# Where the matmul operands lie in SBUF, modulo 256 bytes: level with the weights, or 64 bytes behind them

## The chip, the cores and the metric

The kernel runs on one core of a Trainium2 chip. A core has a matrix engine (TensorE, in the profile PE for the matmuls and PEld for the loads of their stationary operands), VectorE (DVE), ScalarE (ACT), GpSimd (POOL) and DMA queues, here those of SyncE (SP), which bring the weights from device memory into SBUF, the on-chip memory of 128 partitions. An address in this text is a byte offset within each partition. The metric is the device time of one execution in microseconds (us), the median over runs.

## The reference, cut to what matters

The reference is a decoder trunk of two layers on 256 positions of width 2048, in float32. Each layer has a mixer and a dense feed-forward with hidden width 8192, each wrapped in norms and a residual:

```
for layer in range(2):
    y = rmsnorm(h, norm_w[layer, 0])
    y = linear_attention_mixer(y, ...) if layer == 0 else spatial_gating_mixer(y, ...)
    h = h + rmsnorm(y, norm_w[layer, 1])
    y = square(relu(rmsnorm(h, norm_w[layer, 2]) @ w_up)) @ w_down
    h = h + rmsnorm(y, norm_w[layer, 3])
```

The mixer of layer 0 projects 2048 to 8208 columns, runs a gated delta rule and a retention on 8 heads each, and projects back. The mixer of layer 1 projects 2048 to 8192 columns, gates the halves against each other over blocks of 128 positions (a LayerNorm and eight 128x128 matrices) and projects 4096 back to 2048. Nearly all the arithmetic is in the products with the large weights.

## The kernel before, in words

**Products of float32 in three matmuls.** Every float32 operand of a large product is split in two: `hi`, rounded to the engine's reduced float32 form (float32r), and `lo`, the rest. A product is hi·hi + lo·hi + hi·lo, three matmuls that add into one PSUM bank (lines 138 to 140, 324 to 326 and 368 to 370). For each matmul the engine first loads a 128x128 stationary operand (its first argument, PEld in the profile), then streams the moving operand (its second argument) of 256 or 512 columns through the array. Each matmul of these lines has a load of its own, and the load for the next matmul runs while the present one streams.

**Weights.** `weights` (line 121) brings a unit of 128x2048 numbers, 1 MB, by one DMA into a tile `raw`, ScalarE copies it rounded into `whi` (line 131), and VectorE writes the rest to `wlo` (line 132). There are 3 buffers of `raw` and 4 each of `whi` and `wlo`, 8192 bytes in a partition each.

**Three kinds of large product.**

- `chunk_tok` (line 161): activations stationary, 128 positions at a time, and 512 columns of weights moving (`prod_tok`, lines 138 to 140). All projections of the mixers, part of the down projection of the feed-forwards and the first chunk of each up projection go this way. In layer 0 a few products have 400, 384 or 256 columns. With 400 columns (line 500, `spans0`) a unit holds four blocks of 1600 bytes, and block j of the moving weights begins 64·j bytes (modulo 256) behind the first.
- `up_pass` (line 313): weights stationary, and all 256 positions of the normed activations `xh`, `xl` moving (lines 324 to 326). Fifteen of the sixteen chunks of each up projection go this way.
- `chunk7` (line 355): 512x512 blocks of the down projection by seven half-size products in place of eight (sums of operand blocks are formed on VectorE), with the hidden activations `e0`, `e1` or their sums `f0`, `f1` stationary and 256 columns of weights or weight sums moving (lines 368 to 370). One `chunk7` has 7·2·3 = 42 matmuls, and 37 of them run in each feed-forward.

**Between the stages.** `down_last` (line 256) finishes a sub-layer: it adds the last products, norms, adds to the residual `h`, and writes the input of the next sub-layer, transposed and split, into eight tiles `xh0` to `xh3`, `xl0` to `xl3` of pool `xp`. `new_x` (line 207) takes these tiles; each has 4 k-tiles of 256 positions, 4096 bytes.

**Where tiles lie.** Pools are laid one behind the other: `gap` (one tile of `PAD0` bytes, only there to move what follows), `wp` (weights), `cp` (small constants, beginning with a second tile of `PAD1` bytes), `xp` (normed activations), `hp` (residual and accumulators), and then the pool of the running stage: `l0`, `ffn1`, `sg`, `ffn3`. In the program as built, modulo 256 bytes: `raw`, `whi` and `wlo` begin at 0; all `xh`, `xl` at 0; the feed-forward's `e0`, `e1`, `f0`, `f1`, `qsum`, `rl`, `tr` at 0; in layer 1's mixer `v0` to `v7` at 128 and `e0` to `e3` at 0; in layer 0's mixer `kq`, `Bn`, `PT` at 0 and `Um0`, `Um1` at 224. Slices that the matmuls take out of these tiles begin at multiples of 512 bytes in them, except in the products of 400 columns. In layer 1's mixer the tiles `v0` to `v7` hold the value half first and are then used again, beside `e0` to `e3`, for the gated activations that are the stationary operands of the output projection.

**Order.** The order within each engine comes from the code above and the tile framework's scheduler; tensors wait for each other by semaphores.

Of the kernel before, what the change touches and what calls it, by code (L numbers as in the profile page):

```python
# [10 lines left out]
F32 = mybir.dt.float32  # L11
F32R = mybir.dt.float32r
# [5 lines left out]
P = 128  # L18
D = 2048
SEQ = 256  # L20
# [9 lines left out]
PARTS = [4, 2, 1, 1]  # L30
WAIT = [26, 30]
AHEAD = 200
PAD0, PAD1 = 896, 544
WARM = 10
SEVEN, KEPT = (0, 1, 2), 1
ORDER = (None, 0, None, 1, None, 2, None, 3)
# [59 lines left out]
def program(tc, nc, A, S):  # L96
# [3 lines left out]
    xp = tc.alloc_tile_pool(name="xp", bufs=1)  # L100
# [5 lines left out]
    V, G, ACT, PE, DMA = nc.vector, nc.gpsimd, nc.scalar, nc.tensor, nc.sync  # L106
    uid = [0]
    ahead = [0]

    V.memset(gap.tile([P, PAD0 // 4], F32, tag="gap0", name="gap0"), 0.0)  # L110
    V.memset(cp.tile([P, PAD1 // 4], F32, tag="gap1", name="gap1"), 0.0)

    def T(pool, shape, tag, dt=F32, bufs=None):
        uid[0] += 1
        kw = {} if bufs is None else {"bufs": bufs}
        return pool.tile(shape, dt, tag=tag, name=f"{tag}_{uid[0]}", **kw)
# [81 lines left out]
            ACT.activation(hi, src, AF.Copy, scale=col)  # L198
            V.scalar_tensor_tensor(lo, src, col, hi.bitcast(F32), ALU.mult, ALU.subtract)

    def group(pool, th, tl, bufs=None):
        return T(pool, [P, 4, SEQ], th, F32R, bufs), T(pool, [P, 4, SEQ], tl, F32R, bufs)

    def kts(groups):
        return [(e[0][:, j, :], e[1][:, j, :]) for e in groups for j in range(4)]

    def new_x(n=4):
        return [group(xp, f"xh{g}", f"xl{g}") for g in range(n)]

    def to_channels(src, dst, b, col=None):  # L210
        tp = bank(tpp, 512, "tp")
# [28 lines left out]
    h = [[None] * 4 for _ in range(2)]  # L240
# [14 lines left out]

    def down_last(s, X, rows, w1, w0, yw, rpend):
        units = [weights(s, [(r, [(c * 512, 512)]) for r in rows]) for c in range(4)]
        newx = None if w0 is None else new_x()
        rh = [None, None]
        rv = [None, None]  # L260
        for b in range(2):
            ssy = small(4, "ssy")
            yb = yw(b)
            for c in range(4):
                ps = bank(acc, 512, "acc")
                for j in range(4):
                    prod_tok(ps, X[j], b, units[c], j, 512, j == 0, j == 3)
                yt = y[b][c]
                V.tensor_tensor(yt, ps, yt, ALU.add)  # L269
                square_sum(ssy[:, c : c + 1], yt)  # L270
                (V if c == 3 else G).tensor_tensor(yb[c], yt, w1[c], ALU.mult)  # L271
                if c == 2:
                    base = small(1, "base")
                    V.tensor_reduce(base, ssy[:, 0:3], AX.X, ALU.add)
                    V.tensor_scalar(base, base, 1.0 / D, EPS if rpend is None else rpend[b], ALU.mult, ALU.add)
            rs = small(1, "rs")
            V.tensor_scalar(rs, ssy[:, 3:4], 1.0 / D, base, ALU.mult, ALU.add)
            rsqrt(rs, rs)
            for c in range(4):
                ht = h[b][c]  # L280
                V.scalar_tensor_tensor(ht, yb[c], rs, ht, ALU.mult, ALU.add)  # L281
                if w0 is None:
                    DMA.dma_start(A["out"][b * P : (b + 1) * P, c * 512 : (c + 1) * 512], ht)
                else:
                    (V if c == 0 else G).tensor_tensor(yb[c], ht, w0[c], ALU.mult)
                    to_channels(yb[c], newx[c], b)
        if w0 is not None:
            for b in range(2):
                ssh = small(4, "ssh")
                for c in range(4):  # L290
                    square_sum(ssh[:, c : c + 1], h[b][c])
                rh[b] = T(cp, [P, 1], f"rh{b}", bufs=2)
                tot = small(1, "tot")
                V.tensor_reduce(tot, ssh, AX.X, ALU.add)
                var = small(1, "var")
                V.tensor_scalar(var, tot, 1.0 / D, EPS, ALU.mult, ALU.add)
                rsqrt(rh[b], var)
                rv[b] = T(cp, [P, 1], f"rv{b}", bufs=2)
                V.tensor_scalar(rv[b], var, var, EPS, ALU.mult, ALU.mult)
            newx = kts(newx)  # L300
        return newx, rh, rv
# [81 lines left out]
    def ffn(up, dn, X, rh, w1i, w0i):  # L383
        last = HID // 512 - 1
        with tc.tile_pool(name=f"ffn{w1i}", bufs=1, reuse_waits="tile") as fp:

            def pair(name):
                return T(fp, [P, 4, SEQ], f"{name}h", F32R), T(fp, [P, 4, SEQ], f"{name}l", F32R)

            def relu2(ps):  # L390
                r = T(fp, [P, 512], "rl", bufs=3)
# [65 lines left out]
            t = []  # L457
# [36 lines left out]
    def layer0_mixer():  # L494
        rstd = [T(cp, [P, 1], f"rh{b}", bufs=2) for b in range(2)]
        s = S["la_in"]
        with tc.tile_pool(name="l0", bufs=1, reuse_waits="tile") as lp:
            xg = new_x()
            X = kts(xg)
            spans0 = [(4096, 16), (3072, 384)]  # L500
            ps = [bank(acc, 400, "acc") for _ in range(2)]
# [512 lines left out]
    def layer1_mixer(X, rh):  # L1014
        si, so = S["sg_in"], S["sg_out"]
        with tc.tile_pool(name="sg", bufs=1, reuse_waits="tile") as gp:
            ws = T(gp, [P, 8, P], "ws")
            DMA.dma_start(ws, A["ws"].rearrange("p (g t) -> p g t", t=P))
            G.affine_select(ws, ws, pattern=[[0, 8], [1, P]], compare_op=ALU.is_ge, fill=0.0, base=0,
                            channel_multiplier=-1)  # L1020
            v = [None] * 8
            st = [T(gp, [P, 8, 6], f"st{b}") for b in range(2)]

            def v_evac(c, b, ps):
                if v[c] is None:
                    v[c] = T(gp, [P, 2, 512], f"v{c}")
                ACT.activation(v[c][:, b, :], ps, AF.Gelu_apprx_tanh, scale=rh[b])
                V.bn_stats(st[b][:, c, :], v[c][:, b, :])

            for b, ps in first_chunk(si, X, [(SGW, 512)]):  # L1030
                v_evac(0, b, ps)
            for c in range(1, 8):
                ps = chunk_tok(si, X, ALLK, [(SGW + c * 512, 512)], 512)
                for b in range(2):
                    v_evac(c, b, ps[b])
            rs, mu = [], []
            for b in range(2):
                mv = T(gp, [P, 2], f"mv{b}")
                V.bn_aggr(mv, st[b])
                var = small(1, "var")  # L1040
                V.tensor_scalar(var, mv[:, 1:2], EPS, None, ALU.add)
                r = T(gp, [P, 1], f"lr{b}")
                rsqrt(r, var)
                rs.append(r)
                mu.append(mv[:, 0:1])

            tags = ["e0", "e1", "e2", "e3", "v0", "v1", "v2", "v3", "e0", "e1", "e2", "e3", "v4", "v5", "v6", "v7"]
            gts = [None] * 8

            def gate(g):  # L1050
                wb = T(hp, [P, 512], "bc", bufs=4)
                DMA.dma_start(wb, A["lnw"][:, g * 512 : (g + 1) * 512].partition_broadcast(P))
                bb = T(hp, [P, 512], "bc", bufs=4)
                DMA.dma_start(bb, A["lnb"][:, g * 512 : (g + 1) * 512].partition_broadcast(P))
                pss = []
                for b in range(2):
                    t = v[g][:, b, :]
                    V.tensor_scalar(t, t, mu[b], rs[b], ALU.subtract, ALU.mult)
                    G.tensor_tensor(t, t, wb, ALU.mult)
                    G.tensor_tensor(t, t, bb, ALU.add)  # L1060
                ps = chunk_tok(si, X, ALLK, [(g * 512, 512)], 512)
                us = []
                for b in range(2):
                    pm = bank(mxp, 512, "mx")
                    PE.matmul(pm, ws[:, g, :], v[g][:, b, :], start=True, stop=True)  # L1065
                    u = T(gp, [P, 512], "u", bufs=2)
                    ACT.activation(u, ps[b], AF.Gelu_apprx_tanh, scale=rh[b])
                    V.scalar_tensor_tensor(u, pm, bsc[:, g : g + 1], u, ALU.add, ALU.mult)
                    us.append(u)
                dst = (T(gp, [P, 4, SEQ], tags[2 * g], F32R), T(gp, [P, 4, SEQ], tags[2 * g + 1], F32R))  # L1070
                for b in range(2):
                    blocks_split(T(hp, [P, 512], "bc", bufs=4), us[b], dst, b)
                gts[g] = kts([dst])

            def rows(g):
                return [g * 512 + j * P for j in range(4)]

            gate(0)
            for a in (0, 2, 4):
                gate(a + 1)  # L1080
                gate(a + 2)
                down(so, gts[a] + gts[a + 1], rows(a) + rows(a + 1), a == 0)
            gate(7)
            down(so, gts[6], rows(6), False)

            def rows_in(tags):
                t = [T(gp, [P, 2, 512], g) for g in tags]
                return [t[0][:, 0], t[0][:, 1], t[1][:, 0], t[1][:, 1]]

            w1 = row_load(rows_in(["v0", "v1"]), "nrow", 2)  # L1090
            w0 = row_load(rows_in(["v2", "v3"]), "nrow", 6)
            return down_last(so, gts[7], rows(7), w1, w0, lambda b: rows_in(["e0", "e1"]), None)
# [62 lines left out]
```

## Time and profile before

| | |
|---|---|
| median of 2 runs | 2518.86 us (2517.79 to 2519.94) |
| profiled execution | 2520.84 us, span 2519.1 us |
| granted TensorE clock, mean | 0.998 |
| PE busy | 2485.1 us, 99% of the span, 15418 matmuls |
| PEld busy | 2234.5 us, 89% |
| DVE / ACT / POOL busy | 1984.7 (79%) / 1260.5 (50%) / 183.2 us (7%) |
| DMA | 480.17 MB, mean 191 GB/s |

A busy share is the part of the span in which an engine worked. The end of a matmul in this profile is modelled, and a row's mean duration of a matmul is longer than the time from its start to the start of the next: matmuls overlap in the pipeline. What a stream of matmuls costs is read from the starts.

By time the program runs as follows: layer 0's mixer until about 565 us, its feed-forward until about 1250 us, layer 1's mixer until about 1815 us, its feed-forward until the end.

### The profile page before, as it was taken

The numbers are of one execution on the slowest core, as the hardware profiler recorded it, in microseconds if no ns is written. First come the engines' busy times: TensorE is split into PE (matmuls) and PEld (weight loads), VectorE is DVE, ScalarE is ACT, GpSimd is POOL, SyncE is SP. The second block draws the span as 40 slices with busy tenths as digits, with TensorE's granted clock in tenths as the row PEclk, the third lists the DMA queues.
The fourth block names the chain that finished last, engine by engine and source line by source line (L and its number), as shares of the span: only waits on it lengthen the run. The fifth ranks groups of instructions, "written<-read, shape, count | busy, mean of one in ns | idle before, by whom it ended". The sixth has DMA issues, their size and how long they took to land.

```text
span 2519.1 us, 37114 instructions
## 1 busy us (share of the span) xinstructions
PE 2485.1 (99%) x15418; PEld 2234.5 (89%) x15418; DVE 1984.7 (79%) x2322; ACT 1260.5 (50%) x1266; POOL 183.2 (7%) x144
## 2 busy tenths in 40 slices
PE   9999999999999999999999999999999999999998
PEld 8788888879999999999878878888799999999997
DVE  6586855578898889889864596876888988988897
ACT  6655444455455545455554434333555545555553
POOL 0001201130000000000210110110300000000001
PEclk9999999999999999999999999999999999999999
DMA  8444544644554555555455455555445555555553
GB/s 310 164 154 152 191 157 175 213 159 184 204 190 180 197 200 193 192 202 203 182 218 188 181 208 209 196 197 200 151 185 202 189 194 201 201 184 184 201 203 132
DMA packets 81832, 480.17 MB, mean 191 GB/s; under 512 B 13696, under 2 KB 15872, under 8 KB 27392
## 3 DMA queue, kind: packets, MB, share of 16 engines
q1 hardware_dynamic: 81664, 477.80, 52.5%
q8 instruction: 121, 1.98, 0.3%
q14 instruction: 47, 0.39, 0.0%
HBM read 475.14 MB, written 2.62 MB: 190 GB/s over the span
## 4 chain that ended last, share of the span: by engine, by line
PE 46%; DVE 3%; POOL 1%; issue 0%; ACT 0%; DVEq 0%; POOLq 0%; ACTq 0%
PE acc L138 8%; PE acc L140 8%; PE acc L139 8%; PE tp L326 5%; PE tp L325 5%; PE tp L324 5%; PE acc L368 1%; PE acc L370 1%; PE acc L369 1%; PE mx L370 1%; PE mx L369 1%; PE mx L368 1%; DVE h L281 1%; DVE wlo L132 1%; PE mx L1065 1%
## 5 line engine op out<-in xcount | busy, mean ns | idle before, releaser
L132 DVE TENSOR_TENSOR wlo<-raw,whi 128x2048 fp32r<-128x2048 f32 (+3 forms) x366 | 824.8, 2256 | 264.4 <-ACT whi L131 254.9
L131 ACT ACTIVATE whi<-raw 128x2048 fp32r<-128x2048 f32 (+3 forms) x366 | 686.4, 1876 | 469.9 <-PE acc L139 286.8
L326 PE MATMUL tp<-xh,wlo 128*128 128x256 f32 x1920 | 543.5, 283 | 0.0
L325 PE MATMUL tp<-xl,whi 128*128 128x256 f32 x1920 | 543.3, 283 | 0.0
L324 PE MATMUL tp<-xh,whi 128*128 128x256 f32 x1920 | 543.1, 283 | 0.0
L138 PE MATMUL acc<-whi,xh 128*128 128x512 f32 (+3 forms) x1120 | 439.3, 392 | 3.2 <-ACT whi L131 3.2
L140 PE MATMUL acc<-wlo,xh 128*128 128x512 f32 (+3 forms) x1120 | 431.5, 386 | 1.8 <-DVE wlo L132 0.9
L139 PE MATMUL acc<-whi,xl 128*128 128x512 f32 (+3 forms) x1120 | 431.8, 385 | 0.0
L324 PEld LDWEIGHTS tp<-xh,whi 128*128 128x128 f32 x1920 | 368.4, 192 | 1.7
L325 PEld LDWEIGHTS tp<-xl,whi 128*128 128x128 f32 x1920 | 368.4, 192 | 1.7
L326 PEld LDWEIGHTS tp<-xh,wlo 128*128 128x128 f32 x1920 | 368.4, 192 | 0.0
L138 PEld LDWEIGHTS acc<-whi,xh 128*128 128x128 f32 x1120 | 211.2, 189 | 43.5 <-ACT whi L131 4.4
L140 PEld LDWEIGHTS acc<-wlo,xh 128*128 128x128 f32 x1120 | 210.7, 188 | 42.9 <-DVE wlo L132 2.9
L195 ACT ACTIVATE whi<-qsum 128x2048 fp32r<-128x2048 f32 x74 | 141.7, 1915 | 210.4 <-DVE qsum L349 166.7
L139 PEld LDWEIGHTS acc<-whi,xl 128*128 128x128 f32 x1120 | 211.3, 189 | 38.7 <-issue 1.0
L196 DVE TENSOR_TENSOR wlo<-qsum,whi 128x2048 fp32r<-128x2048 f32 x74 | 169.4, 2290 | 66.1 <-ACT whi L195 66.1
L195 ACT ACTIVATE whi<-raw 128x1536 fp32r<-128x1536 f32 x74 | 110.2, 1489 | 184.5 <-DMA raw<-dn 70.2
L431 DVE TENSOR_TENSOR y<-acc,y 128x512 f32<-128x512 f32 x136 | 92.3, 686 | 56.0 <-PE acc L370 54.8
L196 DVE TENSOR_TENSOR wlo<-raw,whi 128x1536 fp32r<-128x1536 f32 x74 | 129.6, 1751 | 2.4 <-ACT whi L195 2.3
L271 POOL TENSOR_TENSOR e0h<-y,f1h 128x512 f32<-128x512 f32 x8 | 13.0, 1648 | 1364.8 <-DVE y L269 1364.8
L138 PE MATMUL acc<-whi,e0h 128*128 128x512 f32 x256 | 100.0, 391 | 0.0
L139 PE MATMUL acc<-whi,e0l 128*128 128x512 f32 x256 | 100.0, 391 | 0.0
(357 smaller groups left out, 4347.6 us busy)
## 6 DMA issues: line engine op xcount, KB each, us to landing
raw<-up SPq DMA_DIRECT2D x128, 1024.0 KB, 4.8
raw<-dn SPq DMA_DIRECT2D x128, 1024.0 KB, 4.8
raw<-sg_in SPq DMA_DIRECT2D x64, 1024.0 KB, 4.8
raw<-la_in SPq DMA_DIRECT2D x56, 1024.0 KB, 4.8
raw<-sg_out SPq DMA_DIRECT2D x32, 1024.0 KB, 4.8
raw<-la_out SPq DMA_DIRECT2D x16, 1024.0 KB, 4.7
raw<-la_in SPq DMA_DIRECT2D x4, 768.0 KB, 8.2
kq<-xT SPq DMA_DIRECT2D x8, 256.0 KB, 6.3
```

What stands on the lines that cost most here:

```text
L131: ACT.activation(a, r, AF.Copy)
L132: V.tensor_tensor(d, r, a.bitcast(F32), ALU.subtract)
L138: PE.matmul(ps, xh, wh, start=first, stop=False)
L139: PE.matmul(ps, xl, wh, start=False, stop=False)
L140: PE.matmul(ps, xh, wl, start=False, stop=last)
L195: ACT.activation(hi, src, AF.Copy)
L196: V.tensor_tensor(lo, src, hi.bitcast(F32), ALU.subtract)
L324: PE.matmul(out, wh[:, col], xh, start=k == 0 and m % 2 == 0, stop=False, skip_group_check=True)
L325: PE.matmul(out, wh[:, col], xl, start=False, stop=False, skip_group_check=True)
L326: PE.matmul(out, wl[:, col], xh, start=False, stop=k == NKT - 1, skip_group_check=True)
L368: PE.matmul(ps, x[k][0], wh, start=k == 0, stop=False, skip_group_check=True)
L431: V.tensor_tensor(Y[k, c], p, Y[k, c], ALU.add)
```

## The change: what it does

Only places change. `PAD0` and `PAD1` shrink from 896 and 544 bytes to 128 and 32 (the same modulo 256, so the weights and `xp` still begin at 0). The tiles of `xp` grow by 64 bytes (`xh`) and 192 bytes (`xl`), and the eight views that the matmuls use are cut out of them at an offset: `X_IN` puts all views at 0 modulo 256, `X_UP` all of them at 64. `X_IN` is used for the inputs of the two mixers, `X_UP` for the inputs of the two feed-forwards. In the feed-forwards each pair `e0`, `e1`, `f0`, `f1` gets a spacer of 64 bytes ahead of it and one of 192 bytes behind it, so that these eight tiles begin at 64. In layer 1's mixer two spacers of 128 bytes move `v0` to `v7` from 128 to 0 and leave what lies behind `lr1` where it was. A spacer is a tile that GpSimd sets to zero once (`skip`).

So against the weights, modulo 256, of before and now:

| matmuls | stationary | moving | before | now |
|---|---|---|---|---|
| mixers, activations `xh`, `xl` | activations | weights | level | level |
| feed-forward, `up_pass` | weights | `xh`, `xl` | level | moving 64 behind stationary |
| feed-forward, `chunk7` | `e`, `f` | weights | level | stationary 64 behind moving |
| feed-forward, `chunk_tok`, `down_last`, first chunk | `e`, `xh`, `xl` | weights | level | stationary 64 behind moving |
| layer 1's mixer, `v0` to `v7` in the output projection | `v` | weights | stationary 128 behind moving | level |

```diff
-PAD0, PAD1 = 896, 544
+PAD0, PAD1 = 128, 32
+X_IN, X_UP = (0, 192), (64, 0)
...
+    def skip(pool, n):
+        uid[0] += 1
+        G.memset(pool.tile([P, n // 4], F32, tag=f"skip{uid[0]}", name=f"skip{uid[0]}"), 0.0)
+
...
-    def group(pool, th, tl, bufs=None):
-        return T(pool, [P, 4, SEQ], th, F32R, bufs), T(pool, [P, 4, SEQ], tl, F32R, bufs)
+    def group(g, at):
+        t = T(xp, [P, 1040], f"xh{g}", F32R), T(xp, [P, 1072], f"xl{g}", F32R)
+        return [a[:, o // 4 : o // 4 + 1024].rearrange("p (j t) -> p j t", t=SEQ) for a, o in zip(t, at)]
...
-    def new_x(n=4):
-        return [group(xp, f"xh{g}", f"xl{g}") for g in range(n)]
+    def new_x(at):
+        return [group(g, at) for g in range(4)]
...
-        newx = None if w0 is None else new_x()
+        newx = None if w0 is None else new_x(X_UP if rpend is None else X_IN)
...
             def pair(name):
-                return T(fp, [P, 4, SEQ], f"{name}h", F32R), T(fp, [P, 4, SEQ], f"{name}l", F32R)
+                if name in seen:
+                    return T(fp, [P, 4, SEQ], f"{name}h", F32R), T(fp, [P, 4, SEQ], f"{name}l", F32R)
+                seen.add(name)
+                skip(fp, 64)
+                hi = T(fp, [P, 4, SEQ], f"{name}h", F32R)
+                lo = T(fp, [P, 4, SEQ], f"{name}l", F32R)
+                skip(fp, 192)
+                return hi, lo
+
+            seen = set()
...
-            xg = new_x()
+            xg = new_x(X_IN)
...
             st = [T(gp, [P, 8, 6], f"st{b}") for b in range(2)]
+            skip(gp, 128)
...
                 mu.append(mv[:, 0:1])
 
+            skip(gp, 128)
             tags = ["e0", "e1", "e2", "e3", "v0", "v1", "v2", "v3", "e0", "e1", "e2", "e3", "v4", "v5", "v6", "v7"]
```

The order of instructions on PE, DVE, ACT and SP stays as it was. Only POOL gets more: eight small memsets at the start of each feed-forward and two at the start of layer 1's mixer. On POOL, at the start of the first feed-forward, before the change, `rh` is the last scale that the stage before leaves, and `e0h` the first work at the end of the feed-forward:

```order
L191 TENSOR_TENSOR rh_868_4593<-var_4596,m_3_87 128x1
L191 TENSOR_TENSOR rh_877_4610<-var_4613,m_3_87 128x1
L271 TENSOR_TENSOR e0h_11559<-y_887_4628,f1h_11068 128x512
```

And with the change, in which code lines stand a few lines lower:

```order
L196 TENSOR_TENSOR rh_868_4593<-var_4596,m_3_87 128x1
L196 TENSOR_TENSOR rh_877_4610<-var_4613,m_3_87 128x1
L116 MEMSET skip_4622 128x16
L116 MEMSET skip_4626 128x48
L116 MEMSET skip_4792 128x16
L116 MEMSET skip_4796 128x48
L116 MEMSET skip_4800 128x16
L116 MEMSET skip_4804 128x48
L116 MEMSET skip_5133 128x16
L116 MEMSET skip_5137 128x48
L277 TENSOR_TENSOR e0h_11575<-y_889_4632,f1h_11084 128x512
```

The eight memsets stand between the two, and nothing else has moved there.

## The prediction

> **What bounds the kernel now.** I read the page's first part, then the sums over the two feed-forwards' steady stretches (columns: stretch, length, then busy us and count of PE, PEld, DVE, ACT, POOL, the granted clock, DMA).
>
> ```profile
> span 2519.1 us, 37114 instructions
> PE 2485.1 (99%) x15418; PEld 2234.5 (89%) x15418; DVE 1984.7 (79%) x2322; ACT 1260.5 (50%) x1266; POOL 183.2 (7%) x144
> ```
>
> ```profile
> 577.00:1225.00 648.00, 648.00 (x4905) 625.52 (x4903) 568.29 (x550) 339.86 (x258) 0.00 (x0) 1.00 0.54 195
> 1840.00:2485.00 645.00, 645.00 (x4893) 623.38 (x4893) 565.77 (x543) 338.34 (x258) 0.00 (x0) 1.00 0.53 193
> ```
>
> PE streams without a gap at the full granted clock; DVE is next, with 568 of 648 us. So the time there is the number of matmuls times what one costs, and a change of that price is a change of the time until DVE binds. DVE's idle time in the two stretches, (648.00 − 568.29) + (645.00 − 565.77) = 159 us, is the most that a faster PE could take out of them.
>
> The price is read from starts, at a place where 512 columns give way to 256 (PE rows in order of time: start, modelled duration).
>
> ```profile
> 654.21 0.39 PE L138 MATMUL acc<-whi,e1h 128*128 128x512 f32 x1
> 654.44 0.39 PE L139 MATMUL acc<-whi,e1l 128*128 128x512 f32 x1
> 654.66 0.39 PE L140 MATMUL acc<-wlo,e1h 128*128 128x512 f32 x1
> 654.89 0.28 PE L324 MATMUL tp<-xh,whi 128*128 128x256 f32 x1
> 655.00 0.28 PE L325 MATMUL tp<-xl,whi 128*128 128x256 f32 x1
> ...
> 655.48 0.28 PE L326 MATMUL tp<-xh,wlo 128*128 128x256 f32 x1
> ```
>
> Three matmuls of 512 columns take 654.89 − 654.21 = 0.68 us, 227 ns each; four of 256 take 655.48 − 655.00 = 0.48 us, 120 ns each. The 256 extra columns cost 107 ns, or 0.417 ns a column; 256 columns at that rate are 107 ns and 512 are 213, so either kind pays some 13 ns that are not columns. This rest is what the change can touch: it moves no work, only where the two operands lie against each other.
>
> **Does the place matter at all?** The trace of before holds places that are not level. In layer 0's output projection `Um` begins at 224 and `Bn` at 0; in layer 1's, `v` begins at 128 and `e` at 0; all are stationary against weights at 0, with 512 columns (groups by shape, window 500 to 566 us for the first two rows, whole span for the others; last columns: count, busy us, mean ns).
>
> ```profile
> L139 PE MATMUL acc<-whi,Um 128*128 128x512 f32 x4 | 1.6, 395 | 0.0
> L139 PE MATMUL acc<-whi,Bn 128*128 128x512 f32 x4 | 1.6, 389 | 0.0
> ...
> L139 PE MATMUL acc<-whi,v 128*128 128x512 f32 x128 | 50.6, 395 | 0.0
> L139 PE MATMUL acc<-whi,e 128*128 128x512 f32 x128 | 49.8, 389 | 0.0
> ```
>
> Same line, same shape, 6 ns more at 224 and at 128 than level. So the place costs something, and level is the best of these three.
>
> 64 itself stands once in the trace: in the first products of layer 0, where block j of the weights begins at 64·j and the activations at 0. Each block has six matmuls of 400 columns. The rows are the first of a block, in the order j = 1, 2, 3, 0, 1, 2, 3, and the sixth of the last block:
>
> ```profile
> 18.90 0.34 PE L138 MATMUL acc<-whi,xh 128*128 128x400 f32 x1
> 19.98 0.34 PE L138 MATMUL acc<-whi,xh 128*128 128x400 f32 x1
> 21.08 0.34 PE L138 MATMUL acc<-whi,xh 128*128 128x400 f32 x1
> 22.18 0.34 PE L138 MATMUL acc<-whi,xh 128*128 128x400 f32 x1
> 23.26 0.34 PE L138 MATMUL acc<-whi,xh 128*128 128x400 f32 x1
> 24.35 0.34 PE L138 MATMUL acc<-whi,xh 128*128 128x400 f32 x1
> 25.45 0.34 PE L138 MATMUL acc<-whi,xh 128*128 128x400 f32 x1
> 26.37 0.34 PE L140 MATMUL acc<-wlo,xh 128*128 128x400 f32 x1
> ```
>
> Level (j = 0): 22.18 to 23.26, 1.08 us for six, 180 ns. Moving 64 behind stationary (j = 1): 1.08 + 1.09 us for twelve, 180.8 ns, +0.8. Moving 128 behind (j = 2): 1.10 + 1.10, 183.3 ns, +3.3. Moving 192 behind (j = 3), which modulo 256 is stationary 64 behind moving: 1.10 us for six and 0.92 for five, 183.6 ns, +3.6. The rows have 0.01 us, so each of these is good to about 1 ns.
>
> **The change part by part.** Counts, from the groups of the whole span (the other two lines of each product have the same counts), and the page's row of the copies that each `chunk7` makes once:
>
> ```profile
> L324 PE MATMUL tp<-xh,whi 128*128 128x256 f32 x1920 | 543.1, 283 | 0.0
> L139 PE MATMUL acc<-whi,e0l 128*128 128x512 f32 x256 | 100.0, 391 | 0.0
> L139 PE MATMUL acc<-whi,e1l 128*128 128x512 f32 x176 | 69.4, 394 | 0.0
> ...
> L195 ACT ACTIVATE whi<-qsum 128x2048 fp32r<-128x2048 f32 x74 | 141.7, 1915 | 210.4 <-DVE qsum L349 166.7
> ```
>
> 1. `up_pass`: 3·1920 = 5760 matmuls, moving 64 behind stationary now. By block j = 1, +0.8 ns: **+4.6 us**. Its bounds are those of any matmul here: below, the whole 13 ns gone; above, the 6 ns of `Um`. I take the row of the same offset and direction, though it has 400 columns.
> 2. `chunk7`: 74·42 = 3108 matmuls, stationary 64 behind. By j = 3, +3.6 ns: **+11.2 us**; same bounds.
> 3. 512 columns in the feed-forwards: 3·(256 + 176) on `e`, and 2·16·2·3 = 192 of the first chunks on `xh`, `xl`: 1488 matmuls, stationary 64 behind, +3.6 ns: **+5.4 us**.
> 4. `v` level: 3·128 = 384 matmuls at −6 ns, **−2.3 us**. The matmuls that gate `v` (32 in all) also change places; at 6 ns they are 0.2 us either way, left out.
> 5. Memsets. The two gap tiles that DVE clears at the start get smaller; they took (rows of DVE in order of time, and behind them the page's row of POOL's first work at the end of a feed-forward)
>
> ```profile
> 0.92 0.24 DVE L110 MEMSET gap<- 128x224 f32 x1 [0.92 <-PEq L1103]
> 1.14 0.17 DVE L111 MEMSET gap<- 128x136 f32 x1
> 4.46 0.88 DVE L199 SCALAR_TENSOR_TENSOR xl<-kq,par,xh 128x256 fp32r<-128x256 f32 x2 [3.12 <-ACT xh L198]
> ```
>
> ```profile
> L271 POOL TENSOR_TENSOR e0h<-y,f1h 128x512 f32<-128x512 f32 x8 | 13.0, 1648 | 1364.8 <-DVE y L269 1364.8
> ```
>
> and DVE then waits 3.12 us for ScalarE: their shrinking is worth nothing. The feed-forwards' spacers (16 memsets of 16 or 48 columns) stand on POOL behind the last `rh` and ahead of work for which POOL waited 1364.8 us in all: nothing, even where one waits for the old owner of its memory; no PE or DVE instruction reads a spacer. Were that cover gone, a memset of this size would cost no more than the 0.24 us of L110, 4 us for all. In layer 1's mixer the two spacers stand between the two `rh`; the second `rh` is first read behind 96 matmuls of 227 ns, 22 us later: nothing.
>
> Sum: 4.6 + 11.2 + 5.4 − 2.3 = **+18.9 us**. The profiled execution took 2520.84 us (its span and 1.7 us around it), 2.0 us over the median of 2518.86; 2520.84 + 18.9 − 2.0 gives **2538 us**.
>
> [...]
>
> **The rivals.**
>
> *A, faster: 64 apart takes the two streams out of each other's way where the load runs the whole time.* A load's record is far longer than the period of 120 ns at 256 columns, about as long as the 180 ns at 400, and shorter than the 227 at 512, so the block rows need not carry over. The loads and matmuls of the two shapes (min/median/max ns, `L326` in the first feed-forward, `e` in a window of layer 1):
>
> ```profile
> L326 PEld LDWEIGHTS tp<-xh,wlo x933: 187/192/192, 576.9 to 1219.2; 128*128 128x128 f32 x187
> L326 PE MATMUL tp<-xh,wlo x933: 279/283/283, 577.0 to 1219.3; 128*128 128x256 f32 x187
> L139 PEld LDWEIGHTS acc<-whi,e x64: 187/188/190, 1503.9 to 1546.8; 128*128 128x128 f32 x64
> ```
>
> A load is 192 ns at 256 columns and 188 at 512: here the two do meet more. And the first matmul of 256 columns behind 512 started its successor after 0.11 us (654.89 to 655.00), not 0.12: level, but with no load from before still under way. So some 6 ns of the 13 hang on how the streams meet, and another place may free them. Against it: j = 1 and j = 3 show nothing of the kind. Price: 6 ns less on 5760 + 3108 = 8868 matmuls is −53 us, with part 4 −55: **2464 us**; 3 ns less would give 2490. At 13 ns it would be −115, still under DVE's 159.
>
> [...]
>
> *B, slower: the load becomes what paces 256 columns.* In the steady stretch the load already fills the whole period, so a place that also lengthens the load adds to every matmul, where at 512 columns it stays hidden. For it: 192 against 188 ns, and three of the four places off level cost 3 to 6 ns even with slack. Priced at the 6 ns of `Um` on 8868 + 1488 matmuls it is +62, less 2.3: **2579 us**. It decides (2%, 50.4 us) from 5.2 ns a matmul on.
>
> *C, the places do nothing at 256 columns:* only parts 3 and 4 remain, +3: **2522 us**. For it, that all 256-column groups have the same 283 ns whatever DVE and ACT do; against it, `Um` and `v`. It is also what would be left if the offsets cancelled; but 4160 + 4288 bytes of an `xh`, `xl` pair are 33·256, so all four groups stay at 64.
>
> **How the numbers follow.** Forecast, by the rows of the same offset: 0.35, with its own range of 2525 to 2555. A: 0.33, from 2430 to 2495, most of it near 2464. B: 0.18. C: 0.14. About 2%, 50 us, is what a measurement of this kernel can tell from no change. Faster by that (below 2468) is the larger part of A: 0.28. Slower (above 2569) is most of B: 0.15. Within: the forecast, C and the rests of A and B: 0.57. The range holds the forecast and C, A down to 2440 and B up to 2580; about 2 in 10 lie outside.
>
> **What would show it.** Starts of `L324` to `L326` in the second profile: 121 ns apart is the forecast, 114 or less A, 126 B, 120 C; the same of `L368` to `L370`, where the forecast has 123 to 124. `e0`, `e1` with 512 columns should be some 231 apart instead of 227, and `v` as `e`. DVE's idle time in the feed-forwards must grow with B and shrink with A. I am wrong in the mechanism if `xh` in the mixers, whose places are unchanged, moves as well, and wrong in the size if 256 columns answer to 64 otherwise than 400 do.

## The result: 35 us faster, and the profile after

The changed kernel takes 2483.78 us (median of 2 runs, 2481.77 to 2485.8), 0.9858 of before with a 95% interval of 0.9837 to 0.9879. That is 35 us less, inside the range of the prediction but on the other side of the forecast of +19. By the bound of 2% it still counts as no change.

The first part of the page after, to be read against the same two lines of before:

```profile
span 2480.0 us, 37131 instructions
PE 2447.2 (99%) x15418; PEld 2191.0 (88%) x15418; DVE 1977.1 (80%) x2322; ACT 1261.5 (51%) x1266; POOL 185.4 (7%) x162
```

The count of matmuls is the same, and TensorE is as full as before. Only its busy time is smaller, by 38 us, nearly all that the span lost (39 us between these two executions, 35 between the medians). The sums over the steady stretches of the two feed-forwards (columns as before: stretch, length, then busy us and count of PE, PEld, DVE, ACT, POOL, the granted clock, DMA):

```profile
577.00:1215.00 638.00, 636.69 (x4928) 609.99 (x4927) 572.34 (x564) 343.16 (x260) 0.00 (x0) 1.00 0.55 199
1810.00:2446.00 636.00, 635.91 (x4964) 611.43 (x4963) 569.97 (x553) 344.20 (x263) 0.00 (x0) 1.00 0.55 200
```

The clock is full (1.00 in both rows), as it was. DVE's idle time is (638.00 − 572.34) + (636.00 − 569.97) = 132 us, where it was 159: a faster TensorE has eaten into it, and DVE still doesn't bind.

The price of a matmul, meaning the time from its start to the next start, is read from the first rows of successive stretches (PE in order of time: start, modelled duration). The stretches that begin with the first four rows hold 48 matmuls of `up_pass` (now lines 330 to 332), 42 of `chunk7` (374 to 376), 48 of `up_pass` and 24 of 512 columns (143 to 145); the last two rows are the start and the end of a later stretch of `up_pass`:

```profile
583.17 0.28 PE L330 MATMUL tp<-xh,whi 128*128 128x256 f32 x1
...
588.83 0.28 PE L374 MATMUL acc<-whi,e0h 128*128 128x256 f32 x1
...
593.60 0.28 PE L330 MATMUL tp<-xh,whi 128*128 128x256 f32 x1
...
599.04 0.39 PE L143 MATMUL acc<-whi,e0h 128*128 128x512 f32 x1
...
604.63 0.28 PE L374 MATMUL mx<-whi,f0h 128*128 128x256 f32 x1
...
630.69 0.28 PE L330 MATMUL tp<-xh,whi 128*128 128x256 f32 x1
...
636.13 0.28 PE L374 MATMUL acc<-whi,e1h 128*128 128x256 f32 x1
```

- `up_pass`: (588.83 − 583.17)/48 = 117.9 ns.
- `chunk7`: 4.77/42 = 113.6 ns.
- `up_pass` again, the same lines on the next of the four pairs `xh`, `xl`: (599.04 − 593.60)/48 = 113.3 ns.
- 512 columns: 5.59/24 = 232.9 ns.
- `up_pass` on the same pair as in the first row (the third of four, one chunk later): (636.13 − 630.69)/48 = 113.3 ns.

Before, 256 columns cost 120 in every stretch and 512 columns 227. So the price at 64 is not one number, not even on the same tiles. Over the whole trace the unbroken stretches run at either 113.3 or 117.8 ns and at nothing between: of `up_pass` 58 at the lower price and 60 at the higher, of `chunk7` 58 and 18. But for the first groups of each feed-forward, which one it is follows a fixed cycle. Behind 512 columns come 118 (`up_pass`), 113 (`chunk7`), 113 (`up_pass`), then either the next 512 columns, which start the cycle anew, or 118 (`chunk7`), 118 (`up_pass`), 113, 113. In `up_pass` this cycle runs nearly in step with the four pairs: of the 114 stretches that are one whole pair, the first and the third pair have the higher price and the second and the fourth the lower, in all but six. The tiles of a pair take 8448 bytes, so every second pair lies 256 bytes off modulo 512, and one might take the price for a matter of the place modulo 512. The six speak against it (the third pair has both prices above), and so do the fourth scan below, where one tile has both, and the run with `xh`, `xl` alone at 64, where all pairs cost the same.

The ledger, from the sums of starts to starts in the two traces: `up_pass` −24.2 us (mean 115.7 ns), `chunk7` −16.7 (114.6), `e0` and `e1` with 512 columns +4.2, `v` −1.7. The four make −38.5 of the span's −39.1. (The two means leave out the few spacings over 150 ns.) The +4.2 is not the price alone: without the few spacings over 260 ns, which hold the waits, the mean went from 227.8 to 233.0, some +6.7 us on 1296 matmuls, and this execution waited less at these lines than that of before. In a second trace of the changed kernel (the run of `after5` below) where those long spacings add up as before the change (9.9 and 10.1 us, here 5.3), the sum is +6.6.

The groups by shape that answer to those of before (last columns: count, busy us, mean ns):

```profile
L330 PE MATMUL tp<-xh,whi 128*128 128x256 f32 x1920 | 533.5, 278 | 0.0
L144 PE MATMUL acc<-whi,e0l 128*128 128x512 f32 x256 | 101.1, 395 | 0.0
L144 PE MATMUL acc<-whi,v 128*128 128x512 f32 x128 | 49.9, 390 | 0.0
```

`up_pass` went from 283 to 278, `e0l` from 391 to 395, and `v` from 395 to 390, the level value. The load (min/median/max ns of `up_pass`'s third line, whole span):

```profile
L332 PEld LDWEIGHTS tp<-xh,wlo x1920: 187/188/190, 565.7 to 2442.9; 128*128 128x128 f32 x192
```

The load was 192 ns at this shape (median, before) and is 188, what it takes at 512 columns (the row of `e` before: 188).

The memsets: the eighteen spacers on POOL (min/median/max ns), and POOL's wait ahead of its first work at the end of a feed-forward:

```profile
L116 POOL MEMSET skip<- x18: 108/124/142, 554.6 to 1797.2; 128x16 f32 x8, 128x48 f32 x8, 128x32 f32 x2
L277 POOL TENSOR_TENSOR e0h<-y,f1h 128x512 f32<-128x512 f32 x8 | 13.1, 1653 | 1327.8 <-DVE y L275 1327.8
```

The spacers are 18 of 124 ns, 2.2 us in all, and behind them POOL still waits 1327.8 us.

### The profile page after: what moved, and what is told of

Read it like the earlier page. It is cut to its first block, busy times and chain, and to the rows that moved or that the text cites. A ratio compares the mean times of both kernels' runs of the same rounds, so it can differ in the third digit from the quotient of the medians.

```text
span 2480.0 us, 37131 instructions
## 1 busy us (share of the span) xinstructions
PE 2447.2 (99%) x15418; PEld 2191.0 (88%) x15418; DVE 1977.1 (80%) x2322; ACT 1261.5 (51%) x1266; POOL 185.4 (7%) x162
## 4 chain that ended last, share of the span: by engine, by line
PE 46%; DVE 3%; POOL 1%; issue 1%; ACT 0%; DVEq 0%; POOLq 0%; ACTq 0%
PE acc L145 8%; PE acc L143 8%; PE acc L144 8%; PE tp L331 4%; PE tp L330 4%; PE tp L332 4%; PE acc L374 1%; PE acc L375 1%; PE acc L376 1%; PE mx L376 1%; PE mx L375 1%; PE mx L374 1%; DVE wlo L137 1%; DVE h L287 1%; PE mx L1082 1%
## 5 line engine op out<-in xcount | busy, mean ns | idle before, releaser
L331 PE MATMUL tp<-xl,whi 128*128 128x256 f32 x1920 | 533.5, 278 | 0.0
L330 PE MATMUL tp<-xh,whi 128*128 128x256 f32 x1920 | 533.5, 278 | 0.0
L332 PE MATMUL tp<-xh,wlo 128*128 128x256 f32 x1920 | 533.3, 278 | 0.0
L330 PEld LDWEIGHTS tp<-xh,whi 128*128 128x128 f32 x1920 | 360.6, 188 | 2.1
L331 PEld LDWEIGHTS tp<-xl,whi 128*128 128x128 f32 x1920 | 360.2, 188 | 1.9
L332 PEld LDWEIGHTS tp<-xh,wlo 128*128 128x128 f32 x1920 | 360.0, 188 | 0.0
L277 POOL TENSOR_TENSOR e0h<-y,f1h 128x512 f32<-128x512 f32 x8 | 13.1, 1653 | 1327.8 <-DVE y L275 1327.8
L145 PE MATMUL acc<-wlo,e0h 128*128 128x512 f32 x256 | 101.2, 395 | 0.0
```

Of the source, the lines that this page charges most:

```text
L145: PE.matmul(ps, xh, wl, start=False, stop=last)
L330: PE.matmul(out, wh[:, col], xh, start=k == 0 and m % 2 == 0, stop=False, skip_group_check=True)
L331: PE.matmul(out, wh[:, col], xl, start=False, stop=False, skip_group_check=True)
L332: PE.matmul(out, wl[:, col], xh, start=False, stop=k == NKT - 1, skip_group_check=True)
```

## Experiments: is it the place, and is the price one number?

Two theories stood after the result. The first: the load of one matmul's stationary operand and the stream of another's moving operand meet in SBUF inside TensorE's own work, and the distance of the two addresses modulo 256 bytes sets what this costs. The second: other engines, which write and read the same memory, meet TensorE's accesses differently now. The scans below leave the whole trunk out; they only issue matmuls, with the granted clock at 1.00 and no instruction of another engine in their long part.

**TensorE alone, one operand moved at a time.** The kernel holds level tiles `flat` and `big` and sixteen tiles that begin at 0, 16, ... 240 modulo 256. Behind twelve level matmuls of 512 columns come 48 of 256 columns with the moving operand at an offset; the same again with the stationary operand there; last, 32 of 512 columns with the stationary operand there.

```diff
+for o in range(0, 256, 16):
+    lead()
+    ...    # 48 times: stationary level, moving tiles[o], 256 columns
+    lead()
+    ...    # 48 times: stationary tiles[o], moving level, 256 columns
+    ...    # 32 times: stationary tiles[o], moving level, 512 columns
```

> A kernel of its own that leaves the whole trunk out and copies x to the output: only TensorE works in its long part. Per place d (0, 16, ... 240 bytes modulo 256) it runs 48 matmuls of 256 columns with the moving operand at d and the stationary at 0, then the same with the stationary at d and the moving at 0, each behind 12 level matmuls of 512 columns; then 32 of 512 columns with the stationary at d. Theory 1 (the load and the stream of TensorE meet in SBUF, by their distance alone): at 256 columns 120 ns a matmul level and 113 or 118 ns at 64, in both directions, as in the changed kernel; at 512 columns 227 level, about 231 to 234 at 64, 128 and 224, as in both kernels' traces; moving at d behaves as stationary at 256 - d. Theory 2 (the gain needs VectorE, ScalarE or DMA traffic at those places): every place the same, 120 and 227 ns. If theory 1 holds, the question is whether some place does better than 113 ns at 256 columns, or is good for 256 and 512 at once.

PE in order of time, equal matmuls in one row with their count; `at064x` is the tile at 64, `L66` has it moving, `L74` stationary with 256 columns, `L80` stationary with 512:

```profile
25.41 5.92 PE L66 MATMUL half<-at000x,flat 128*128 128x256 f32 x48
31.16 2.91 PE L51 MATMUL lead<-big,flat 128*128 128x512 f32 x12
...
59.16 5.82 PE L66 MATMUL half<-at064x,flat 128*128 128x256 f32 x48
64.82 2.92 PE L51 MATMUL lead<-big,flat 128*128 128x512 f32 x12
...
84.59 5.64 PE L66 MATMUL half<-at112x,flat 128*128 128x256 f32 x48
90.07 2.91 PE L51 MATMUL lead<-big,flat 128*128 128x512 f32 x12
...
236.25 5.91 PE L74 MATMUL half<-big,at144x 128*128 128x256 f32 x48
241.99 2.92 PE L51 MATMUL lead<-big,flat 128*128 128x512 f32 x12
...
292.36 7.44 PE L80 MATMUL full<-big,at000x 128*128 128x512 f32 x32
299.64 7.42 PE L80 MATMUL full<-big,at016x 128*128 128x512 f32 x32
...
321.82 7.62 PE L80 MATMUL full<-big,at064x 128*128 128x512 f32 x32
329.28 7.58 PE L80 MATMUL full<-big,at080x 128*128 128x512 f32 x32
```

256 columns, moving at 0: 5.75 us for 48, 120 ns; at 64: 5.66, 118; at 112: 5.48, 114. 512 columns, stationary at 0: 7.28 us for 32, 227 ns; at 64: 7.46, 233. No other engine works, and the three prices 120, 118 and 233 of the real kernels are all there. The second theory isn't needed for them. The first theory holds in its first half only: the price hangs on the places, but not on their distance alone. With the stationary operand off level, 256 columns cost 118 at 64 as well, but 120 at 144 (5.74 us for 48), the same distance modulo 256 as that of moving at 112, which costs 114. That it is the load and the stream which meet, and that they meet in SBUF, no run here shows. No place is clearly worse than level at 256 columns (114 to 120 ns moving, 117 to 120 stationary, level 120). At 512 columns 0, 16 and 240 are the cheapest here (227) and the rest cost 230 to 234; but in the second scan below, behind matmuls of 256 columns, 16 costs 233 as well, so a place doesn't fix the price of 512 columns either.

With every other engine idle the place alone moved a matmul from 120 to 114 ns, and from 227 to 233. Whether another engine makes PE wait is not tested here.

**One half of the change at a time.** First only the normed activations at 64, with `e`, `f` and `v` as before. Against the changed kernel:

```diff
-                skip(fp, 64)
...
-                skip(fp, 192)
...
-            skip(gp, 128)
...
-            skip(gp, 128)
```

> Only the normed activations of the two feed-forwards are moved to 64; e, f stay level and v stays at 128. Theory 1: up_pass goes from 120 to 113 to 118 ns by stretches, 5760 matmuls, -23 us (-13 if all stretches take 118, -38 if all take 113); chunk7 stays at 120, the 512-column products on e at 227, the 192 of the first chunks pay 4 to 7 ns, +1 us. Time about 2496 us, ratio 0.991. Theory 2: the gain came with the places of e, f, against their writers: then no gain here, 2519 us, ratio 1.000.

Measured: 2509.72 us, 0.9958 of before (0.9941 to 0.9974), a gain of 10 us. The starts at the first stretches shown above:

```profile
585.29 0.28 PE L330 MATMUL tp<-xh,whi 128*128 128x256 f32 x1
...
590.95 0.29 PE L374 MATMUL acc<-whi,e0h 128*128 128x256 f32 x1
...
595.99 0.28 PE L330 MATMUL tp<-xh,whi 128*128 128x256 f32 x1
```

`up_pass` takes 5.66 us for 48, 117.9 ns, and it does so in all of its 118 stretches; `chunk7`, level, 5.04 for 42, 120.0. The lower price does not occur.

Then only `e`, `f` at 64, the normed activations and `v` as before:

```diff
-X_IN, X_UP = (0, 192), (64, 0)
+X_IN, X_UP = (0, 192), (0, 192)
...
-            skip(gp, 128)
...
-            skip(gp, 128)
```

> Only e0, e1, f0, f1 are moved to 64; the normed activations stay level in all stages, v at 128. Theory 1: chunk7 goes from 120 to 113 to 118 ns, 3108 matmuls, -16 us (-7 to -21); the 1296 matmuls of 512 columns on e pay 4 to 7 ns, +6 us; up_pass stays at 120. Time about 2509 us, ratio 0.996. Theory 2: all of the change's gain is here, 2484 us, ratio 0.986. The two single changes and v (-2 us) should add up to the -35 us of the whole under theory 1, unless which of 113 and 118 a stretch takes depends on the stretch before.

Measured: 2518.5 us, 0.9995 (0.9986 to 1.0005), no change.

```profile
582.83 0.28 PE L330 MATMUL tp<-xh,whi 128*128 128x256 f32 x1
...
588.57 0.28 PE L374 MATMUL acc<-whi,e0h 128*128 128x256 f32 x1
...
593.52 0.28 PE L330 MATMUL tp<-xh,whi 128*128 128x256 f32 x1
```

`up_pass` has 5.74/48 = 119.6 ns and `chunk7` 4.95/42 = 117.9; only 3 of the 76 stretches of `chunk7` run at 113. The 512 columns cost 233.5 ns. In the sums of starts that is +4.3 us against the −6.9 of `chunk7`.

Both expectations were too good, since they gave each half its share of the whole gain; the second had named the exception, a price that hangs on the stretch before. The halves are worth 10 and 2 us, `v` 2 (its own sum above), 14 of 35 together, each time with an interval of a few us. The other 21 us or so come only when both operands are at 64: only then does half of the stretches fall from 118 to 113. That is 58 stretches of 48 and some 55 more of 42 by 4.5 ns, 12.5 + 10.4 = 23 us. The sums of starts say the same: `up_pass` −24.2 us with both moved and −11.9 with its own half, `chunk7` −16.7 and −6.9, which leaves 22 us for the two together.

**Does the low price come from the order of the streams alone?** TensorE alone again, with both operands off level: for all 256 pairs of places in steps of 16 bytes, 12 matmuls of 512 columns, then twice 30 with the moving operand at one place and 30 with the stationary at the other.

```diff
+for x_at in range(0, 256, 16):
+    for e_at in range(0, 256, 16):
+        full(tiles[e_at], 12)
+        for _ in range(2):
+            up(tiles[x_at])       # 30, moving at x_at
+            seven(tiles[e_at])    # 30, stationary at e_at
```

> A kernel of its own that leaves the whole trunk out and copies x to the output. For each pair of places (normed activations at x, hidden activations at e, both 0, 16, ... 240 modulo 256; weights at 0) it runs what a feed-forward runs: 12 matmuls of 512 columns with the stationary at e, then twice 30 of 256 columns as in up_pass (moving at x) and 30 as in chunk7 (stationary at e), without a gap. Theory 1a (the price of a stretch hangs on its own distance and on the phase that the stretch before it hands over): at x = e = 64 the four stretches take 118, 113, 113, 118 ns as in the changed kernel; at x = 64, e = 0: 118, 120, 118, 120; at x = 0, e = 64: 120, 118, 120, 118; level 120 in all. Rival 1b (113 and 118 come from the other engines' traffic, or from which tiles and chunks of the kernel it is): at x = e = 64 all four stretches the same, 118. If 1a holds, the best pair is read from here; 113.3 in all four stretches would be the most that was ever seen, 120 is what level pays.

At (64, 64) the four stretches cost 117.7, 117.8, 117.7 and 113.5 ns. Both prices are there without any other engine, but not in the order expected. With one of the two level the results are those of the half changes: (64, 0) 117.8 and 120, (0, 64) 119.8 and 117.9. No pair of the 256 has the low price in all four stretches.

The stretches of that scan were shorter than the kernel's. So a third one took the kernel's own lengths and order of one feed-forward group, for 64 pairs in steps of 32 bytes:

```diff
-            full(tiles[e_at], 12)
+            full(e, 24)
+            for down in (seven, seven, seven, full, seven, full, seven, full):
+                up(x, 48)
+                down(e, 24 if down is full else 42)
```

> TensorE alone again; it leaves the whole computation out. For each of 64 pairs of places (moving x, stationary e, in steps of 32 bytes) it issues the matmuls of one group of a feed-forward with the kernel's own lengths and order: 24 of 512 columns, then eight times 48 of 256 columns (moving at x) followed by 42 of 256 columns (stationary at e) or by 24 of 512. If the price of a stretch hangs on nothing but the order of the loads and streams before it, the pair (64, 64) repeats the changed kernel: 118 ns for the first 48, then 113, 113, 118, 118, 113, 113, and 118 again behind every 512; a mean of 115.7 and 114.6 ns. If other engines or the exact memory decide which price a stretch takes, the pair has the two prices in another order. (0, 0) has to show 120 throughout. A place worth trying in the kernel would have a mean of 114 ns or less over both kinds, with 512 columns at no more than 230.

The rows of (64, 64), from the start of its group, behind 24 matmuls of 512 columns at 64:

```profile
1692.08 5.81 PE L63 MATMUL half<-at064x,flat 128*128 128x256 f32 x48
1697.73 5.11 PE L70 MATMUL half<-big,at064x 128*128 128x256 f32 x42
1702.68 5.82 PE L63 MATMUL half<-at064x,flat 128*128 128x256 f32 x48
1708.34 4.93 PE L70 MATMUL half<-big,at064x 128*128 128x256 f32 x42
1713.11 5.61 PE L63 MATMUL half<-at064x,flat 128*128 128x256 f32 x48
```

The second stretch takes 4.95/42 = 117.9 ns where the kernel's cycle has 113; the fourth takes 4.77/42 = 113.6. The whole group reads 118, 118, 118, 113, 113, 118, 118 | 118, 113, 113 | 118, 113, 113, the strokes standing for 512 columns. Its later parts are the kernel's cycle exactly, its first part is not, so the expectation held in half. What stood ahead of that first part was different, too.

**What hands the price on?** A fourth scan holds both places at 64 and varies lengths. Each group starts from 24 level matmuls of 512 columns, then come `f` of 512 columns with the stationary operand at 64, and `u`, `c`, `u`, `c`, `u` of 256.

```diff
+plans = [(24, n, 42) for n in range(40, 57)] + [(n, 48, 42) for n in range(16, 33)] + [(24, 48, n) for n in range(34, 51)]
+for f, u, c in plans:
+    full(S, 24)
+    full(e, f)
+    for _ in range(2):
+        up(x, u)
+        seven(e, c)
+    up(x, u)
```

> TensorE alone, all computation left out, both places at 64. A group is 24 matmuls of 512 columns level, 24 of 512 columns with the stationary operand at 64, then 48, 42, 48, 42, 48 matmuls of 256 columns (moving at 64, stationary at 64, in turn). In the first 17 groups the 48 is replaced by 40 to 56, in the next 17 the second 24 by 16 to 33, in the last 17 the 42 by 34 to 50. If the price of a stretch (113 or 118 ns) is a state that the stream carries along and the length of a stretch decides what it hands on, then the prices of the second and later stretches change with these lengths, in a regular way. If the price depends only on the kinds that follow each other, all 51 groups show the same row of five prices. The first stretch behind 512 columns should be at 118 in all of them, unless the number of the 512s counts too.

Two groups that differ in one matmul, 24 or 25 of 512 columns:

```profile
956.96 5.76 PE L51 MATMUL full<-big,at064x 128*128 128x512 f32 x24
962.56 5.82 PE L63 MATMUL half<-at064x,flat 128*128 128x256 f32 x48
968.21 4.94 PE L70 MATMUL half<-big,at064x 128*128 128x256 f32 x42
972.98 5.61 PE L63 MATMUL half<-at064x,flat 128*128 128x256 f32 x48
978.43 5.12 PE L70 MATMUL half<-big,at064x 128*128 128x256 f32 x42
983.38 5.82 PE L63 MATMUL half<-at064x,flat 128*128 128x256 f32 x48
...
994.51 6.00 PE L51 MATMUL full<-big,at064x 128*128 128x512 f32 x25
1000.35 5.81 PE L63 MATMUL half<-at064x,flat 128*128 128x256 f32 x48
1006.00 5.11 PE L70 MATMUL half<-big,at064x 128*128 128x256 f32 x42
1010.94 5.82 PE L63 MATMUL half<-at064x,flat 128*128 128x256 f32 x48
1016.60 4.94 PE L70 MATMUL half<-big,at064x 128*128 128x256 f32 x42
1021.37 4.81 PE L63 MATMUL half<-at064x,flat 128*128 128x256 f32 x41
```

With 24: 5.65/48 = 118, 4.77/42 = 114, 5.45/48 = 114, 4.95/42 = 118, and 118 for the last. This is the kernel's cycle, 118, 113, 113, 118, 118. With 25: 118, 4.94/42 = 118, 5.66/48 = 118, 4.77/42 = 114, and 113 for the last. All seventeen numbers from 16 to 32 obey it: every even one gives the first row of prices, every odd one the second. Of the other lengths, 41, 47 and 53 of `u` give the second row of prices and most give the first. Other rows come up only where a matmul at the seam of two stretches takes some 220 ns in place of 113 or 118, and that happens every 6 in length: at 43, 44, 49, 50, 55 and 56 of `u` and at 37, 38, 43, 44, 49 and 50 of `c` (38, 44 and 50 have 118, 113, 118, 113, 118). Away from the seams each stretch of all 51 groups has one of the two prices, and the first behind the 512s is always at 118. So the price of a stretch is a state that TensorE's own stream carries from stretch to stretch, and the kernel's cycle is what its numbers 24, 48 and 42 make of it. What this state is inside the engine, and why a seam costs more at some lengths, stays open; no record of the trace shows it.

**Other places in the whole kernel.** By the scans two other pairs might do as well or better: activations and `e`, `f` both at 192, or at 192 and 32. Against the changed kernel (the tiles' sizes and spacers follow the two numbers):

```diff
-X_IN, X_UP = (0, 192), (64, 0)
+X_AT, E_AT = 192, 192    # the other run: 192, 32
+X_IN, X_UP = (0, 256 - X_AT), (X_AT, 0)
...
-                skip(fp, 64)
+                skip(fp, E_AT)
...
-                skip(fp, 192)
+                skip(fp, 256 - E_AT)
```

The changed kernel ran beside them once more:

> The changed kernel again, as the yardstick for the two other places on the same chip: 0.986 of before.

Measured: 2484.87 us, 0.986 (0.9843 to 0.9876), with the cycle as before.

> The whole changed kernel with the feed-forward's activations 192 behind the weights instead of 64, and e, f at 192 instead of 64. If the order of the streams alone sets the prices, TensorE's sum from the run with it alone (5760, 3108 and 1296 matmuls at 115.6, 114.2 and 232.1 ns for this pair, 116.1, 115.1 and 233.3 ns for 64, 64) is 7 us under that of 64, 64, and against what the changed kernel really shows (115.7, 114.6, 232.8) 2 to 3 us: 2476 to 2484 us, 0.983 to 0.986 of before. If other work on the chip picks the price of a stretch, it may be 118 in all of them, and the time 2496 to 2500 us (0.992).

Measured: 2482.14 us, 0.9853 (0.9838 to 0.9867).

```profile
583.50 0.28 PE L331 MATMUL tp<-xh,whi 128*128 128x256 f32 x1
...
588.97 0.28 PE L375 MATMUL acc<-whi,e0h 128*128 128x256 f32 x1
...
593.73 0.28 PE L331 MATMUL tp<-xh,whi 128*128 128x256 f32 x1
...
599.39 0.40 PE L144 MATMUL acc<-whi,e0h 128*128 128x512 f32 x1
```

Behind 512 columns it is now 5.47/48 = 114, 4.76/42 = 113, 5.66/48 = 118: the cycle is shifted by one stretch, and the share of the low price is nearly the same.

> The same with 192 and 32. Alone, TensorE had 113.4 ns in every up_pass stretch and 118.3 in every chunk7 with this pair, with no change from stretch to stretch. If that holds in the kernel, up_pass gains 5760 times 2.3 ns, 13 us, on the changed kernel, chunk7 loses 3108 times 3.7 ns, 11 us, and the 512 columns 1 us: 2478 to 2486 us. If other work picks the price, up_pass shows 113 and 118 in turn here too: 2490 to 2500 us.

Measured: 2485.56 us, 0.9865 (0.9851 to 0.988).

```profile
621.14 0.29 PE L331 MATMUL tp<-xh,whi 128*128 128x256 f32 x1
...
626.62 0.28 PE L375 MATMUL acc<-whi,e1h 128*128 128x256 f32 x1
...
631.58 0.29 PE L331 MATMUL tp<-xh,whi 128*128 128x256 f32 x1
```

Here the cycle is gone: `up_pass` has the low price in 117 of 118 stretches (5.48/48 = 114 with the first matmuls, 113.4 behind them), `chunk7` always the high one (4.96/42 = 118). The mean of `up_pass` fell to 113.9 ns, −10.6 us against the changed kernel, that of `chunk7` rose to 118.3, +11.4 us. Both times came out inside what the scan of the streams alone had given. None of the three places beats another by more than the intervals; the two others are as good as the changed kernel, not better.

## Why the prediction was wrong

The bound was right: TensorE paces the feed-forwards, and the time moved by the price of a matmul times their number, with DVE off the path. What failed is the price. That the time still lies in the predicted range is no merit of the sum: the range had been made wide enough for rival A.

- **Parts 1 and 2, the step that failed.** For the price at 64 the sum took "the row of the same offset and direction, though it has 400 columns", +0.8 and +3.6 ns. At 256 columns level itself is among the dearest places, and 64 costs 2 to 7 ns less in either direction. Measured −24.2 us for +4.6, and −16.7 for +11.2. Why level is dear at 256 columns stays open. The prediction's last sentence named this ("if 256 columns answer to 64 otherwise than 400 do"), and the sum went by the other rows all the same. The 400-column rows were read rightly; they speak of a shape with a longer period (180 ns level, where 256 columns have 120), and the scan shows that 512 and 256 columns answer to the same place with opposite signs (+6 and −2 ns).
- **A step that was not there.** Every case of the prediction gave a place one price. It has two, 113.3 and 117.8 ns, and in the fourth scan the stream before decides between them (24 or 25 matmuls of 512 columns); some 21 of the 35 us come from that alone, and at 64 nearly all of them only with both operands moved. No row of before could show it, since level has 120 ns in every stretch.
- **Part 3** was right in sign and too small in price: 233 ns in the steady stretches for the forecast 231. The measured +4.2 on `e0` and `e1` lies near the forecast +5.4 only because this execution waited less there; at the steady price `e0` and `e1` alone make +6.7.
- **Part 4**: −2.3 forecast, −1.7 measured; `v` is level with `e` now.
- **Part 5** cost nothing, as forecast: DVE waits for ScalarE behind its two memsets (3.41 us now, 3.12 before), POOL behind its own.
- **Rival A** had the right sign, nearly the right size, and a chance of 0.33. Its mechanism, that the load and the stream get out of each other's way, is not shown. The hint that it went by, a load of 192 ns at 256 columns against 188 at 512, did change: the load is 188 now. But the load is no measure of the price. It is 188 at both prices, and in the scan also with the moving operand at 96, where a matmul costs 120 as level. Its price of 6 ns was near the 5.4 of `chunk7` and above the 4.3 of `up_pass`, and it let go of the +4.2 of the 512 columns, so 2464 was too low. "3 ns less would give 2490" lay nearer. What spoke against it, the blocks j = 1 and 3, was read from the same rows of 400 columns.
- **Rival B** had the wrong sign: the load got shorter off level, 188 ns for 192, not longer. (By its own numbers it decides from 5.1 ns a matmul on, not 5.2.) **Rival C** fell with the first row of starts.
- The mixers' `xh`, which the prediction used as a control, did not move: with 512 columns their median is 227 ns from start to start before and after.
- The bound of parts 1 and 2 from below, the whole 13 ns gone, was not reached: the lowest steady price of 256 columns in these runs is 113.3 ns, 6.7 under level.

## What to carry to other kernels

Where TensorE streams without a gap, the places of its two operands modulo 256 bytes were worth 3 to 6% of a matmul here, in either direction, and the sign depended on the number of columns (off level 114 to 120 ns for 120 at 256, 227 to 234 for 227 at 512): measure it at the shape in question, for both operands together. A scan with TensorE alone is cheap (the first took 414 us), and its prices came back in the whole kernel, if not always in the same order; half changes need not add up (10, 2 and 2 us here, and 35 together). A price read from one steady stretch may not be the price of the next one (113.3 and 117.8 ns on the same line here), so count stretches before multiplying.

## What the runs showed that was not expected

- The same line on the same tiles has two steady prices, 113.3 and 117.8 ns, and one matmul of 512 columns more or less (24 or 25) ahead of them swaps which of the later stretches gets which.
- In column times (0.417 ns, an estimate from the prediction's two shapes, 227 and 120 ns) the overhead on top of the columns comes in steps of 16: level pays 13.3 ns, 32 column times, at both shapes; the low price of 256 columns pays 6.7, 16; 512 columns at 64 pay 20, 48. The 117.8 and the prices of several other places (116.7 to 119.2 in the scan) stand between the steps. This is a regularity of the numbers, not an explanation.
- Level, which was the best of the three places that the trace of before shows at 512 columns, is among the worst of sixteen at 256, together with 80, 96 and 128 of the moving operand (120 ns).
